# Last layer's first MLP product by pairs of tiles, seven block products each (Strassen's scheme), in a two-layer fp32 transformer step

## The chip, the core and the metric

The kernel runs on one core of a Trainium2 chip. The metric is the device time of one execution in microseconds (us): three executions of the kernel before gave 1744.67, 1745.09 and 1748.14, a median of 1745.09. Engines are named as in the profile: PE (matmul), PEld (its weight loads), DVE (VectorE), ACT (ScalarE), POOL (GpSimd) and SP (which issues the weight loads from HBM).

## The reference, cut to what matters

Two layers of a hybrid attention and gated-linear-attention block act on 640 columns of activations: 512 latent columns and 128 prompt columns, model width 1024. All is fp32. The end of each layer is an MLP of width 4096; the change is in its first product, in the last layer:

```
h = rmsnorm(x, g_mlp[l]) * (1 + sc2) + sh2
x = x + ga2 * mlp(h, w_up[l], w_down[l])

def mlp(h, w_up, w_down):
    return jnp.square(jax.nn.relu(h @ w_up)) @ w_down
```

## The kernel before, in words

**Tiles.** Activations lie transposed: eight row chunks of 128 partitions, each 640 columns wide (T, line 19). A weight unit is one load of 128x1024 fp32 (512 KB). An "up" unit is w_up for 128 of the 4096 hidden rows, all eight chunks of the contraction. A "dn" unit is w_down for 512 hidden rows (four up tiles) and 256 output rows. The last layer has 32 units of each kind.

**Three products for one.** To keep fp32 accuracy every operand is split into a rounded part and a remainder, and `mm3` (line 547) issues three matmuls for each product: rounded weight by rounded activation, rounded weight by remainder, remainder weight by rounded activation. The 640 columns (642 in an up product, whose last two carry the shift sh2 through the product) are done in two parts, 256 and 384 (or 386), so an up unit is 8 x 3 x 2 = 48 matmuls (`proj`, line 596), and a dn unit twice 24 (`proj4`, line 693), once for each of its 128 output rows.

**Preparing a unit.** `prefetch` (line 421) runs each time a unit has been used (`used`, line 490). It issues the next load on SP while fewer than NRAW = 3 raw tiles (wr) are held, and prepares the next raw tile while fewer than NHL = 3 prepared tiles (wh, wl) are held: ACT copies it to the rounded wh, POOL subtracts to make the remainder wl.

**Around the MLP of the last layer.** `layer` (line 867) ends with the output projection ("o" units). As each row chunk of x gets its last contribution (`resid`, DVE), `late_chunk` (line 836) scales it by G into the rounded row (ACT) and the remainder row (DVE), and adds its square to sqa (ACT, then DVE). PE sums sqa over partitions (ps_ss, in `late_stat`, line 853) and ACT makes rstd2 of it, the factor that is multiplied in when an up product leaves PSUM. The first two up tiles are run side by side (`proj_two`, line 577), the others one by one. An up tile leaves PSUM by `up_evac` (line 1569): DVE multiplies by rstd2 into r, ACT applies the shift and the relu and squares to uh, DVE makes the remainder ul. Buffers r have four turns. PSUM holds two tiles "mm" of two banks and four tiles "sm" of one; accumulators take them in turn.

**Order.** `unit_order` (line 377) sets it: in the MLP four up units, then the four dn units that use the four up tiles before them, and so on. PE's order is the order of the code; on the other engines a scheduler places the instructions by priority, and each engine runs its own in that order.

Of the kernel before, what the change touches and what calls it, by code (L numbers as in the profile page):

```python
# [20 lines left out]
TX = T + 2  # L21
NS = 512
L = 2
# [188 lines left out]
class Kern:  # L212
# [4 lines left out]
    EVP = 600  # L217
    HALF = ((0, 256), (256, T))
# [7 lines left out]
    def run(self):  # L226
        nc, a, ctx = self.nc, self.a, self.ctx
        self.cp = cp = ctx.enter_context(self.pool("const"))
        self.rp = ctx.enter_context(self.pool("rows"))
# [24 lines left out]
        self.cos = cp.tile([128, NS], F32, name="cos")  # L254
        self.sin = cp.tile([128, NS], F32, name="sin")
# [3 lines left out]
        self.cbc = cp.tile([128, 2, D], F32, name="cbc")  # L259
        self.ones = cp.tile([128, 128], F32, name="ones")  # L260
        self.blk_r = cp.tile([128, 128], F32R, name="blk_r")
        self.wg = cp.tile([128, L, 2, 256], F32, name="wg")
        self.xs = self.dp.tile([KC, 128, T], F32, name="xs")
        self.mod = {l: cp.tile([128, 6, KC, 2], F32, name=f"mod{l}") for l in range(L)}
        self.lateh = False
# [7 lines left out]
        self.raw, self.hl, self.over = {}, {}, set()  # L273
        self.rot, self.nacc = False, 0
# [102 lines left out]
    def unit_order(self):  # L377
# [8 lines left out]
        for l in range(L):  # L386
# [34 lines left out]
    def prefetch(self, ahead=650):  # L421
        nc = self.nc
        with self.tc.high_priority(offset=ahead):
            go = True
            while go:
# [35 lines left out]
                if self.raw and self.wprep - self.wused < (self.NHL if self.wx is None else self.NHL + 1):  # L461
                    j = min(self.raw)
                    wx = self.wx is not None and self.wprep == self.NHL
                    t = self.raw.pop(j)
                    if wx:
                        h, lo = (self.wx.tile([128, 1024], F32R, name=n) for n in ("wxh", "wxl"))
                    else:
                        h = self.wp.tile([128, 1024], F32R, name="wh", tag="wh", bufs=self.NHL)
                        lo = self.wp.tile([128, 1024], F32R, name="wl", tag="wl", bufs=self.NHL)
                    self.est.ready[t.name] = max(self.est.ready[t.name], self.dv.t)  # L470
                    nc.scalar.activation(out=h, in_=t, func=AF.Copy)
                    if self.wx is not None:
                        nc.vector.tensor_tensor(out=lo, in0=t, in1=h.bitcast(F32), op=ALU.subtract)
                    elif self.units[j] in self.units[max(0, j - 4):j] + self.units[j + 1:j + 5]:

                        nc.vector.tensor_tensor(out=lo[:, :448], in0=t[:, :448], in1=h[:, :448].bitcast(F32), op=ALU.subtract)
                        nc.gpsimd.tensor_tensor(out=lo[:, 448:], in0=t[:, 448:], in1=h[:, 448:].bitcast(F32), op=ALU.subtract)
                    else:
                        nc.gpsimd.tensor_tensor(out=lo, in0=t, in1=h.bitcast(F32), op=ALU.subtract)
                    self.hl[j] = (h, lo)  # L480
                    self.wprep += 1
                    go = True
# [7 lines left out]
    def used(self, i):  # L490
        self.over.add(i)
        if self.units[i][0] == "ada":
            self.nada -= 1
        elif self.units[i][0] != "z":
# [28 lines left out]
    def acc(self, n=T):  # L523
        t = self.mmp.tile([128, 1024], F32, name="ps_mm", tag="mm")
        return (t[:, 256:512], t[:, 512:256 + n]), [(t[:, 256:256 + n], 0, n)]

    def acc_sm(self, n=T):
        self.dv.take("sm", 2)
        a, b = (self.smp.tile([128, 512], F32, name="ps_sm", tag="sm") for _ in range(2))
        return (a[:, 0:256], b[:, 0:n - 256]), [(a[:, 0:256], 0, 256), (b[:, 0:n - 256], 256, n)]  # L530
# [16 lines left out]
    def mm3(self, ps, wh, wl, hh, hl, first, last, halves=(0, 1), shared=None):  # L547

        nc = self.nc
        for i, (w, h) in enumerate(((wh, hh), (wh, hl), (wl, hh))):  # L550
            for hf in halves:
                lo = self.HALF[hf][0]
# [43 lines left out]
    def proj(self, key, evac):  # L596

        n = TX if self.lateh else T
# [85 lines left out]

    def whole(self, t, segs, np_=128):

        nc = self.nc
        for ap_, lo, hi in segs:
            nc.vector.tensor_tensor(out=t[:, lo:hi], in0=ap_, in1=self.lrstd[0:np_, lo:hi], op=ALU.mult)
# [1044 lines left out]
```

## Time and profile before

| | before |
|---|---|
| three executions, median | 1745.09 us |
| the profiled execution, its own time | 1745.39 us |
| span of the profiled execution | 1743.6 us |
| mean granted clock of PE | 0.979 |
| PE busy, of the span | 95% |
| DVE busy, of the span | 62% |
| ACT busy, of the span | 40% |
| POOL busy, of the span | 36% |

A line of the profile names the tile written, the tiles read, the size and the engine. Nearly all instructions carry one line number, that of a helper, so groups are told apart by tiles. Ends of matmuls are modelled; the time that a matmul takes from the stream is the distance between starts.

### The profile page before, as it was taken

Reading aid. Unit: us, or ns where it says so; the run is one execution under the profiler, and the core shown is the slowest. Engines: PE = TensorE matmul, PEld = TensorE weight load, DVE = VectorE, ACT = ScalarE, POOL = GpSimd, SP = SyncE. Lnnn points to the kernel's source line nnn. Section 1 sums busy time; section 2 is a strip of 40 time slices with the busy share of each in tenths; the row PEclk is TensorE's granted clock in tenths of the full one; section 3 lists DMA queues with packets and bytes.
Section 4 is the critical chain, followed back from the end, with each engine's and each line's share of the span. In section 5 each row is a group of like instructions: output and inputs, shape, how many; then the busy total and the mean of one; then the engine's idle time right before and its main releaser. Section 6 shows DMA issues by size and latency. Waiting matters only on the chain. (4 is left out here: it accounts for less than half of the span.)

```text
span 1743.6 us, 32610 instructions
## 1 busy us (share of the span) xinstructions
PE 1653.4 (95%) x13712; PEld 1575.1 (90%) x13712; DVE 1076.4 (62%) x1971; ACT 703.3 (40%) x1142; POOL 626.7 (36%) x266
## 2 busy tenths in 40 slices
PE   7988788989999999999989899999999999999999
PEld 6977677779999999999988788888999999999998
DVE  5686767788797788777677737586662222222322
ACT  3535335543543233322344445466454223332330
POOL 1234432113334444444345536313233333333331
PEclk9998899999999999999999989999999999999999
DMA  9121233233354454445241111323222222222221
GB/s 369 45 65 64 92 105 119 77 110 121 121 181 139 157 166 134 144 147 169 76 168 51 51 43 57 91 69 94 70 65 84 73 73 73 74 83 74 73 73 73
DMA packets 61345, 179.28 MB, mean 103 GB/s; under 512 B 6928, under 2 KB 17808, under 8 KB 61200
## 3 DMA queue, kind: packets, MB, share of 16 engines
q1 hardware_dynamic: 45360, 159.76, 27.4%
q10 hardware_dynamic: 15840, 17.45, 3.2%
q8 instruction: 108, 1.77, 0.4%
q14 instruction: 37, 0.30, 0.1%
HBM read 170.36 MB, written 6.82 MB: 102 GB/s over the span
## 5 line engine op out<-in xcount | busy, mean ns | idle before, releaser
L197 POOL TENSOR_TENSOR wl<-wr,wh 128x1024 fp32r<-128x1024 f32 (+1 forms) x188 | 490.1, 2608 | 906.0 <-ACT wh L197 856.5
L197 PE MATMUL ps_mm<-row,wh 128*128 128x256 f32 (+1 forms) x2416 | 485.8, 322 | 7.9 <-DVE row L197 3.7
L197 ACT ACTIVATE wh<-wr 128x1024 fp32r<-128x1024 f32 x195 | 206.3, 1058 | 627.7 <-PE ps_sm L197 400.7
L197 PEld LDWEIGHTS ps_mm<-row,wh 128*128 128x128 f32 x2416 | 399.7, 193 | 30.3 <-issue 18.7
L197 PE MATMUL ps_mm<-row,wl 128*128 128x256 f32 (+2 forms) x1208 | 282.7, 313 | 0.5 <-DVE wl L197 0.5
L197 PEld LDWEIGHTS ps_mm<-row,wl 128*128 128x128 f32 x1208 | 224.8, 192 | 0.9 <-DVE wl L197 0.7
L197 DVE SCALAR_TENSOR_TENSOR row<-ps_sm,mod,row 128x256 f32<-128x256 f32 (+1 forms) x216 | 81.8, 432 | 97.0 <-PE ps_sm L197 97.0
L197 DVE SCALAR_TENSOR_TENSOR row<-ps_mm,mod,row 128x128 f32<-128x128 f32 (+2 forms) x180 | 89.4, 536 | 79.2 <-PE ps_mm L197 79.0
L197 DVE SCALAR_TENSOR_TENSOR ar<-ar,cbc 128x1024 f32<-128x1024 f32 x56 | 122.7, 2199 | 0.8
L197 ACT ACTIVATE r<-r 128x640 f32<-128x640 f32 (+2 forms) x192 | 112.3, 617 | 18.6 <-DVE r L197 15.1
L197 PE MATMUL ps_sm<-uh,wh 128*128 128x256 f32 (+1 forms) x512 | 119.2, 309 | 0.0
L197 PE MATMUL ps_mm<-uh,wh 128*128 128x256 f32 (+1 forms) x512 | 119.2, 309 | 0.0
L197 PE MATMUL ps_mm<-ul,wh 128*128 128x256 f32 (+1 forms) x512 | 119.0, 309 | 0.0
L197 PE MATMUL ps_sm<-uh,wl 128*128 128x256 f32 (+1 forms) x512 | 118.9, 309 | 0.0
L197 PE MATMUL ps_sm<-ul,wh 128*128 128x256 f32 (+1 forms) x512 | 118.9, 309 | 0.0
L197 PE MATMUL ps_mm<-uh,wl 128*128 128x256 f32 (+1 forms) x512 | 118.9, 309 | 0.0
L197 PE MATMUL ps_sm<-row,wh 128*128 128x256 f32 (+1 forms) x624 | 118.6, 309 | 0.0
L197 DVE TENSOR_TENSOR ul<-r,uh 128x640 fp32r<-128x640 f32 x64 | 55.2, 862 | 84.5 <-ACT r L197 84.4
L197 DVE TENSOR_TENSOR r<-ps_mm,rstd 128x642 f32<-128x642 f32 x34 | 28.1, 827 | 123.7 <-PE ps_mm L197 123.7
L197 PEld LDWEIGHTS ps_sm<-row,wh 128*128 128x128 f32 x624 | 103.0, 189 | 0.0
L197 PE MATMUL ps_mm<-m,wh 128*128 128x256 f32 (+1 forms) x544 | 102.3, 310 | 0.0
L197 DVE SCALAR_TENSOR_TENSOR r<-ar,cbc 128x1024 bf16<-128x1024 f32 x56 | 93.6, 1689 | 0.0
(203 smaller groups left out, 2947.1 us busy)
## 6 DMA issues: line engine op xcount, KB each, us to landing
wr<-w_dn SPq DMA_DIRECT2D x68, 512.0 KB, 3.5
wr<-w_up SPq DMA_DIRECT2D x64, 512.0 KB, 3.5
ar<-w_ada SPq DMA_DIRECT2D x56, 512.0 KB, 3.7
wr<-w_in SPq DMA_DIRECT2D x48, 512.0 KB, 3.5
wr<-w_ada SPq DMA_DIRECT2D x24, 512.0 KB, 3.5
wa<-w_ada SPq DMA_DIRECT2D x16, 512.0 KB, 10.2
wr<-w_o SPq DMA_DIRECT2D x16, 512.0 KB, 3.5
tab<-bias ACTq DMA_DIRECT2D x32, 96.0 KB, 2.2
```

The costliest lines, as they stand in the source:

```text
L197: r = f(*args, **kw)
```

## The change

Of the 32 up tiles of the last layer the first four stay as they are. The other 28 are taken in 14 pairs. For a pair the two weight units are seen as a 2 x 2 block matrix (two tiles of 128 hidden rows by two halves of the contraction), the activations as 2 x 2 blocks (two halves of the contraction by two halves of the columns, 322 each, for which TX becomes 644), and the product of the two is made with seven block products in place of eight, in Winograd's form of Strassen's scheme.

- `proj_pair` issues the seven products, 12 matmuls of 322 columns each, and combines them on DVE as they leave PSUM (p1, q, r and so on).
- `prepare_part` makes the weights of a pair as four prepared tiles in place of two: the first unit as it lies, two sums S1 and S2 in one tile, the first unit changed in place, and half a tile. Three are 1024 columns wide, the last 512; remainders go to POOL and DVE by turns. Sums are made on DVE.
- `blocks_begin` makes the four combined activation blocks T1 to T4, for four chunk pairs, once, at the start of the last layer's MLP: ACT scales x again into r, DVE subtracts, ACT rounds, DVE makes the remainder.
- In the last layer pairs and dn units alternate (two up units, two dn units); r there has three turns (RBUF).
- In both layers an up product's shift columns move to the two ends of the row, two each, and its two parts are 322 and 322. Constants of the attention move to a pool that is closed before the last MLP. Code of the case `lateh` in the projections, which was never taken there, goes.

```diff
-TX = T + 2
+TX = T + 4
+TH = TX // 2
...
+    PAIRED = (1,)
+    RBUF = (4, 3)
...
+                if l in self.PAIRED and 0 < b < 8:
+                    for i in (0, 2):
+                        for kind, j in (("up", 4 * b), ("dn", 4 * b - 4)):
+                            put(kind, l, j + i)
+                            put(kind, l, j + i + 1)
+                    continue
...
+    def prepare_part(self, j):
...
+            nc.vector.tensor_tensor(out=s1, in0=a21, in1=a22, op=ALU.add)
+            nc.vector.tensor_tensor(out=s2, in0=s1, in1=a11, op=ALU.add)
+
+            self.part = [j, 0, (ta, sums, ta, a22), ((a11, a21), (a12, s2))]
+        j, q, parts, late = self.part
+        if q == 2:
+            for t, u in late:
+                nc.vector.tensor_tensor(out=t, in0=t, in1=u, op=ALU.add)
+        t = parts[q]
+        n = t.free_size()
...
+        nc.scalar.activation(out=h[:, :n], in_=t, func=AF.Copy)
+        eng = nc.vector if q % 2 else nc.gpsimd
+        eng.tensor_tensor(out=lo[:, :n], in0=t, in1=h[:, :n].bitcast(F32), op=ALU.subtract)
...
+    def blocks_begin(self, l, x, mp, rc, rows):
...
+        for k in range(4):
+            b = []
+            for kc in (k, k + 4):
+                t = mp.tile([128, TX], F32, name="r", bufs=self.RBUF[l])
+                for c, e in ((1, 0), (0, T + 2)):
+                    nc.vector.tensor_copy(t[:, e:e + 2], m[:, 3, kc, c:c + 1].to_broadcast([128, 2]))
+                for c, lo, hi in ((1, 0, NS), (0, NS, T)):
+                    nc.scalar.activation(out=t[:, 2 + lo:2 + hi], in_=x[kc][:, lo:hi], func=AF.Copy, scale=self.G[:, kc, c:c + 1])
+                b.append(t)
+            (b11, b12), (b21, b22) = ((hv(t, 0), hv(t, 1)) for t in b)
+
+            for out, y, z in ((b11, b12, b11), (b12, b12, b22), (b22, b22, b11), (b21, b21, b22)):
+                nc.vector.tensor_tensor(out=out, in0=y, in1=z, op=ALU.subtract)
+            for i, t in enumerate((b11, b22, b12, b21)):
+                hh, hl = next(room), next(room)
+                nc.scalar.activation(out=hh, in_=t, func=AF.Copy)
+                nc.vector.tensor_tensor(out=hl, in0=t, in1=hh.bitcast(F32), op=ALU.subtract)
+                self.T[i].append((hh, hl))
+
+    def proj_pair(self, l, i, mp):
...
+        def mul(ps, w, n, rhs):
+            for kc in range(4):
+                ws = slice(512 * n + 128 * kc, 512 * n + 128 * kc + 128)
+                for k, (wv, hv) in enumerate(((w[0], rhs[kc][0]), (w[0], rhs[kc][1]), (w[1], rhs[kc][0]))):
+                    nc.tensor.matmul(ps, lhsT=wv[:, ws], rhs=hv, start=kc == k == 0, stop=kc == 3 and k == 2)
...
+        yield from mul(X, w, 0, B11)
+        with self.tc.high_priority(offset=self.EVP):
+            nc.scalar.activation(out=p1, in_=X, func=AF.Copy)
+        yield from mul(Y, w, 1, B21)
+        tt(ha[0], Y, p1, ALU.add)
...
+        yield from mul(X, w, 0, T2)
+        tt(q, X, p1, ALU.subtract)
+        yield from mul(Y, w, 1, T1)
+        tt(r, Y, q, ALU.add)
...
+        yield from mul(V, w, 0, T3)
+        tt(hb[1], V, r, ALU.add)
+        tt(q, V, q, ALU.add)
...
+        yield from mul(W, w, 1, B22)
+        tt(ha[1], W, r, ALU.subtract)
...
+        yield from mul(V, w, 0, T4)
+        tt(hb[0], V, q, ALU.add)
```

How the order moves, at the three places of which the prediction speaks.

PE, one chunk of one of the last up tiles, before: each product in two parts, rows as they are named in the text above (row_0 is the rounded part of the first chunk, row_1 its remainder).

```order
L197 MATMUL ps_mm<-row_0_13329,wh 128x256
L197 MATMUL ps_mm<-row_0_13329,wh 128x386
L197 MATMUL ps_mm<-row_1_13330,wh 128x256
L197 MATMUL ps_mm<-row_1_13330,wh 128x386
L197 MATMUL ps_mm<-row_0_13329,wl 128x256
L197 MATMUL ps_mm<-row_0_13329,wl 128x386
```

PE, the last pair with the change, from the end of its second block product to the begin of its third.

```order
L198 MATMUL ps_mm<-m_13364,wh 128x322
L198 MATMUL ps_mm<-m_13365,wh 128x322
L198 MATMUL ps_mm<-m_13364,wl 128x322
L198 MATMUL ps_mm<-T_13719,wh 128x322
L198 MATMUL ps_mm<-T_13720,wh 128x322
L198 MATMUL ps_mm<-T_13719,wl 128x322
```

What moved: a chunk's three products of one part stand alone, for one block; a pair has 84 matmuls where two up tiles had 96, and the whole program has 11558 where it had 11726.

DVE, start of the last layer's MLP, before: the last chunk (row_7) gets its contribution, its remainder m, the square sum, and then the first two up tiles leave PSUM (r<-ps_mm).

```order
L197 SCALAR_TENSOR_TENSOR row_7_12735<-ps_sm,mod_108,row_7_12735 128x256 x2
L197 SCALAR_TENSOR_TENSOR row_7_12735<-ps_sm,mod_108,row_7_12735 128x128
L197 SCALAR_TENSOR_TENSOR m_13344<-row_7_12735,G,m_13343 128x512
L197 SCALAR_TENSOR_TENSOR m_13344<-row_7_12735,G,m_13343 128x128
L197 TENSOR_TENSOR sqa<-sqa,sq 128x640
L197 TENSOR_TENSOR r<-ps_mm,rstd_4521 128x642 x2
```

DVE, the same place, with the change: T is a combined block, r<-r a subtraction between scaled chunks, COPY r<-mod the shift columns. The square sum is the row sqa; after the last row shown 17 more rows of these kinds stand before r<-ps_mm of the first up tile.

```order
L198 SCALAR_TENSOR_TENSOR row_7_12755<-ps_sm,mod_111,row_7_12755 128x256 x2
L198 SCALAR_TENSOR_TENSOR row_7_12755<-ps_sm,mod_111,row_7_12755 128x128
L198 TENSOR_TENSOR T_13722<-r,T_13721 128x322
L198 TENSOR_TENSOR T_13724<-r,T_13723 128x322
L198 SCALAR_TENSOR_TENSOR m_13365<-row_7_12755,G,m_13364 128x512
L198 SCALAR_TENSOR_TENSOR m_13365<-row_7_12755,G,m_13364 128x128
L198 TENSOR_TENSOR sqa<-sqa,sq 128x640
L198 COPY r<-mod_111 128x2 x4
L198 TENSOR_TENSOR r<-r 128x322 x3
L198 TENSOR_TENSOR S_13941<-wr 128x512
L198 TENSOR_TENSOR r<-r 128x322
L198 TENSOR_TENSOR S_13941<-S_13941,wr 128x512
```

What moved: two remainders T stand ahead of the last chunk's remainder m, and work on the blocks fills the place between the square sum and the first up tile's way out of PSUM.

ACT, a pair in the steady part of the last MLP, before (one up unit, whose weight copy is wh<-wr, then r and uh of an up tile):

```order
L197 ACTIVATE wh<-wr 128x1024
L197 ACTIVATE r<-r 128x512
L197 ACTIVATE r<-r 128x128
L197 ACTIVATE uh_14121<-r 128x640
L197 ACTIVATE r<-r 128x640
L197 ACTIVATE wh<-wr 128x1024
```

ACT, the same part with the change, one pair; wh<-S is the sums' tile, wh<-wr of 512 columns the last half tile, r<-ps_mm the copy of the first block product out of PSUM. The two wh<-wr of 1024 columns right behind the half tile are the two dn units that follow the pair.

```order
L198 ACTIVATE wh<-wr 128x1024
L198 ACTIVATE r<-ps_mm 128x322
L198 ACTIVATE wh<-wr 128x512
L198 ACTIVATE wh<-wr 128x1024 x2
L198 ACTIVATE r<-r 128x512
L198 ACTIVATE wh<-wr 128x1024
L198 ACTIVATE r<-r 128x128
L198 ACTIVATE uh_14454<-r 128x640
L198 ACTIVATE r<-r 128x640
L198 ACTIVATE r<-r 128x512
L198 ACTIVATE r<-r 128x128
L198 ACTIVATE uh_14485<-r 128x640
```

What moved: the copies for weights stand closer together, and those for the dn units wait for PE inside the pair.

## Rows read from the trace of the kernel before

**Rows 1.** The page's busy time of PE (share of the span, instructions).

```profile
PE 1653.4 (95%) x13712; PEld 1575.1 (90%) x13712; DVE 1076.4 (62%) x1971; ACT 703.3 (40%) x1142; POOL 626.7 (36%) x266
```

**Rows 2.** Busy time by stretch: length, PE, PEld, DVE, ACT, POOL, PEclk, DMA share, GB/s.

```profile
1262.00:1293.00 31.00, 30.52 (x207) 30.07 (x205) 24.97 (x43) 17.18 (x29) 9.62 (x4) 1.00 0.25 81
1429.00:1485.00 56.00, 56.00 (x384) 56.00 (x383) 15.22 (x30) 18.33 (x24) 19.21 (x8) 1.00 0.23 76
```

**Rows 3.** Chain of waits, last MLP: start, length, what ran, matmuls.

```profile
1436.28 7.06 PE ps_sm L197 x48
...
1457.46 3.51 PE ps_mm L197 x24
1460.97 3.52 PE ps_sm L197 x24
```

**Rows 4.** Timeline of PE, first layer's last dn units: start, length, operation.

```profile
884.73 0.28 PE L197 MATMUL ps_sm<-ul,wh 128*128 128x256 f32 x1
...
888.72 0.28 PE L197 MATMUL ps_sm<-uh,wl 128*128 128x256 f32 x1
...
897.06 0.34 PE L197 MATMUL ps_mm<-ul,wh 128*128 128x384 f32 x1
...
905.21 0.34 PE L197 MATMUL ps_mm<-uh,wh 128*128 128x384 f32 x1
```

**Rows 5.** Groups by form from 1293 us on: busy, mean ns, idle before.

```profile
L197 POOL TENSOR_TENSOR wl<-wr,wh 128x1024 fp32r<-128x1024 f32 x61 | 146.5, 2402 | 284.7 <-ACT wh L197 284.7
L197 ACT ACTIVATE wh<-wr 128x1024 fp32r<-128x1024 f32 x61 | 64.7, 1061 | 278.5 <-PE ps_sm L197 206.8 <-PE ps_mm L197 71.7
...
L197 DVE TENSOR_TENSOR r<-ps_sm,rstd 128x386 f32<-128x386 f32 x15 | 8.3, 551 | 0.0
L197 DVE TENSOR_TENSOR r<-ps_sm,rstd 128x256 f32<-128x256 f32 x15 | 6.4, 425 | 39.1 <-PE ps_sm L197 39.1
```

**Rows 6.** DMA issues: operation, count, KB each, median us to landing.

```profile
wr<-w_up SPq DMA_DIRECT2D x64, 512.0 KB, 3.5
```

**Rows 7.** Timeline of DVE around the square sum and the first up tiles.

```profile
1287.82 1.13 DVE L197 SCALAR_TENSOR_TENSOR row<-ps_sm,mod,row 128x256 f32<-128x256 f32 x3
1289.48 1.81 DVE L197 SCALAR_TENSOR_TENSOR m<-row,G,m 128x512 fp32r<-128x512 f32 x2 [0.54 <-ACT m L197]
1291.21 0.81 DVE L197 TENSOR_TENSOR sqa<-sqa,sq 128x640 f32<-128x640 f32 x1
1300.59 0.83 DVE L197 TENSOR_TENSOR r<-ps_mm,rstd 128x642 f32<-128x642 f32 x1 [8.56 <-PE ps_mm L197]
```

**Rows 8.** Timeline of PE there: first up tile, square sum, third up tile.

```profile
1286.13 0.75 PE L197 MATMUL ps_mm<-row,wh 128*128 128x256 f32 x4
...
1292.08 1.34 PE L197 MATMUL ps_ss<-sqa,ones 128*128 128x256 f32 x4 [0.48 <-DVE sqa L197]
...
1302.09 0.75 PE L197 MATMUL ps_mm<-row,wh 128*128 128x256 f32 x4
```

**Rows 9.** Timeline of DVE in the output projection.

```profile
1266.71 2.61 DVE L197 SCALAR_TENSOR_TENSOR row<-row,G,row 128x512 fp32r<-128x512 f32 x2 [0.53 <-ACT row L197]
1269.24 0.81 DVE L197 TENSOR_TENSOR sqa<-sqa,sq 128x640 f32<-128x640 f32 x1
```

**Rows 10.** Timeline of POOL in the output projection, and its slowest remainder in the first layer.

```profile
422.06 3.33 POOL L197 TENSOR_TENSOR wl<-wr,wh 128x1024 fp32r<-128x1024 f32 x1 [0.84 <-ACT wh L197]
...
1266.11 2.40 POOL L197 TENSOR_TENSOR wl<-wr,wh 128x1024 fp32r<-128x1024 f32 x1 [4.65 <-ACT wh L197]
...
1288.07 2.41 POOL L197 TENSOR_TENSOR wl<-wr,wh 128x1024 fp32r<-128x1024 f32 x1 [4.92 <-ACT wh L197]
```

**Rows 11.** Timeline of PE, first layer: waits at the same place, and one of 2.75 us.

```profile
452.23 0.83 PE L197 MATMUL ps_mm<-row,wh 128*128 128x256 f32 x4 [1.48 <-DVE row L197]
458.53 1.34 PE L197 MATMUL ps_ss<-sqa,ones 128*128 128x256 f32 x4 [1.63 <-DVE sqa L197]
...
893.31 0.70 PE L197 MATMUL ps_ss<-sqa,ones 128*128 128x256 f32 x2 [2.75 <-DVE sqa L197]
...
894.02 0.34 PE L197 MATMUL ps_mm<-ul,wh 128*128 128x384 f32 x1
```

**Rows 12.** Timeline of DVE, first layer: two of the shift columns' small operations.

```profile
421.28 0.16 DVE L197 TENSOR_TENSOR row<-mod,row 128x2 fp32r<-128x2 f32 x1
421.36 0.16 DVE L197 CAST row<-mod 128x2 fp32r<-128x2 f32 x1
```

More of the change, by code (lines that the diff above doesn't have):

```diff
@@ L462, in prefetch @@
                     j = min(self.raw)
[L463 to L479, printed above, removed]
@@ L480, in prefetch, with prepare @@
-                    self.hl[j] = (h, lo)
-                    self.wprep += 1
-                    go = True
+                    if self.part is None and not self.paired(self.units[j]):
+                        self.prepare(j)
+                        go = True
+                    elif self.part is not None or j + 1 in self.raw:
+                        self.prepare_part(j)
+                        go = True
+    def prepare(self, j):
+        nc = self.nc
+        wx = self.wx is not None and self.wprep == self.NHL
+        t = self.raw.pop(j)
+        if wx:
+            h, lo = (self.wx.tile([128, 1024], F32R, name=n) for n in ("wxh", "wxl"))
+        else:
+            h = self.wp.tile([128, 1024], F32R, name="wh", tag="wh", bufs=self.NHL)
+            lo = self.wp.tile([128, 1024], F32R, name="wl", tag="wl", bufs=self.NHL)
+        self.est.ready[t.name] = max(self.est.ready[t.name], self.dv.t)
+        nc.scalar.activation(out=h, in_=t, func=AF.Copy)
+        if self.wx is not None:
+            nc.vector.tensor_tensor(out=lo, in0=t, in1=h.bitcast(F32), op=ALU.subtract)
+        elif self.units[j] in self.units[max(0, j - 4):j] + self.units[j + 1:j + 5]:
+            nc.vector.tensor_tensor(out=lo[:, :448], in0=t[:, :448], in1=h[:, :448].bitcast(F32), op=ALU.subtract)
+            nc.gpsimd.tensor_tensor(out=lo[:, 448:], in0=t[:, 448:], in1=h[:, 448:].bitcast(F32), op=ALU.subtract)
+        else:
+            nc.gpsimd.tensor_tensor(out=lo, in0=t, in1=h.bitcast(F32), op=ALU.subtract)
+        self.hl[j] = (h, lo)
+        self.wprep += 1
@@ new lines, in prepare_part @@
+    def prepare_part(self, j):
+        nc = self.nc
+        if self.part is None:
+            ta, tb = self.raw[j], self.raw[j + 1]
+            for t in (ta, tb):
+                self.est.ready[t.name] = max(self.est.ready[t.name], self.dv.t)
+            sums = self.sw.tile([128, 1024], F32, name="S12")
+            a11, a12, a21, a22 = ta[:, 0:512], ta[:, 512:1024], tb[:, 0:512], tb[:, 512:1024]
+            s2, s1 = sums[:, 0:512], sums[:, 512:1024]
+            nc.vector.tensor_tensor(out=s1, in0=a21, in1=a22, op=ALU.add)
[7 more added lines that the diff above has]
+        n = t.free_size()
+        h = self.wp.tile([128, 1024], F32R, name="wh", tag="wh", bufs=self.NHL)
+        lo = self.wp.tile([128, 1024], F32R, name="wl", tag="wl", bufs=self.NHL)
+        nc.scalar.activation(out=h[:, :n], in_=t, func=AF.Copy)
+        eng = nc.vector if q % 2 else nc.gpsimd
+        eng.tensor_tensor(out=lo[:, :n], in0=t, in1=h[:, :n].bitcast(F32), op=ALU.subtract)
+        self.hl[j, q] = (h, lo)
+        self.wprep += 1
+        self.part[1] += 1
+        if q == 2:
+            self.raw.pop(j)
+        elif q == 3:
+            self.raw.pop(j + 1)
+            self.part = None
@@ L488, in unit, with used_part, used @@
         return i, self.hl.pop(i)
-    def used(self, i):
-        self.over.add(i)
-        if self.units[i][0] == "ada":
+    def used_part(self):
+        self.wused += 1
+        self.prefetch()
+    def used(self, *i):
+        self.over.update(i)
+        if self.units[i[0]][0] == "ada":
             self.nada -= 1
-        elif self.units[i][0] != "z":
+        elif self.units[i[0]][0] != "z" and len(i) == 1:
             self.wused += 1
@@ L967, in layer @@
         rows += [tuple(mp.tile([128, TX], F32R, name=f"m{i}{j}", bufs=1) for j in range(2)) for i in range(4)]
-        self.h, self.lateh = rows, True
+        self.h = rows
+        if l in self.PAIRED:
+            self.sw = self.mlp_ctx.enter_context(self.pool(f"blocks{l}", reuse_waits="tile"))
         with self.pool(f"norm2_{l}", 2, reuse_waits="tile") as npl:
@@ L1608, in mlp @@
                 self.ups = []
-            if b < 8:
+            if b < 8 and not self.paired(("up", l, 4 * b)):
                 for i in range(len(self.ups), 4):
```

206 lines of the change are left out of this document (119 added, 87 removed).

## The prediction

> **What bounds the kernel now.** I read the page first: PE is busy 95% of the span [rows 1]. Whether it bounds the stage that is changed is read from the busy times by stretch: between 1429 and 1485 us, four up and eight dn units deep in the last MLP, PE is busy 56.00 of 56.00 us at a granted clock of 1.00, while DVE has 15, ACT 18 and POOL 19 us of work [rows 2]. The chain of waits says the same: from 1293 us to the end it is PE alone, 7.06 us for each up unit (48 matmuls) and 3.51 or 3.52 us for each half of a dn unit (24) [rows 3]. So a matmul taken out of this stage is worth its full time, as long as nothing new makes PE wait. The stage before it is another matter. In the output projection (1262 to 1293 us) DVE is busy 24.97 of 31 us [rows 2], and it is late: the last chunk's contribution starts on DVE at 1287.82 us [rows 7], though PE left the output projection for the first up tile at 1286.13 [rows 8]. PE waits for DVE's square sum at 1292.08 already, for 0.48 us [rows 8]. The change puts new DVE work just there.
>
> **The matmuls.** Matmuls of 256 columns alone start 117.4 ns apart (34 steps from 884.73 to 888.72 us), those of 384 columns 173.4 ns (47 steps from 897.06 to 905.21) [rows 4]. On the line between them 322 columns take 117.4 + 66 x 56.0/128 = 146.3 ns. A pair of up tiles takes 2 x 7.06 = 14.12 us before [rows 3], and 84 x 146.3 ns = 12.29 us after: 1.83 us less, **25.6 us for 14 pairs**. The other bound: today's mixed stream has 7.06 us / 48 = 147.1 ns for a mean of 321 columns; with 147.5 ns for 322, a pair saves 1.73 us, 24.2 in all. I take the line, since the new stream is of one size, as the streams it comes from are. The Trainium skill (TensorE: Matmul & The Clock Gate, section Back-to-back issue gap) gives N/2.4 + 2.5 ns for an isolated gap; by it the pairs would save only 22.4 us, an estimate from that page, and the trace disagrees with it already at 256 columns (109.2 ns against the measured 117.4).
>
> The other 36 up tiles (32 in the first layer, 4 in the last) go from parts of 256 and 386 columns to 322 and 322. By the same line each matmul falls from 147.1 to 146.3 ns: 36 x 48 x 0.8 ns = **1.4 us less**; by the other bound 0.7 us more. The dn units keep their matmuls; that they alternate with pairs moves no work off or onto PE.
>
> **The weights of a pair.** Four prepared tiles in place of two: ACT copies 3.5 tile widths where it copied 2, POOL keeps two remainders of 2.40 us per pair [rows 5], DVE gets the other two, four sums of 512 columns, seven combinations of 322 and two full-width products by rstd2. All lie beside PE if each tile is ready in time. With three prepared tiles, the copy for a tile starts when the tile three places earlier has been used. The shortest lead is that of the first dn unit: its copy waits for the pair's second part, and PE comes to it after the third and fourth, 36 matmuls or 5.27 us later. Copy and remainder take 1.06 + 2.40 = 3.46 us [rows 5], so 1.8 us are left; POOL's slowest remainder in the rows here, 3.33 us [rows 10], would still leave 0.9. A half tile's lead is 7.0 us, the third part's too, the others' are longer. Loads: a pair holds two of the three raw tiles until its third and fourth part are prepared, and the copy of the second dn unit stands 7.1 us behind the end of the third part's preparation (72 matmuls or 10.5 us into the pair, against 3.46), against 3.5 us to landing [rows 6]. DVE's row of work waits in front of the next pair's first sum until its second raw tile lands (some 2 us into the first dn unit), and the last block product's combination stands behind it; nobody needs that result for over 20 us. I take **0**, with an upper bound of 0.5 us per pair, 7 in all: one two-input DVE operation of 0.81 us [rows 7] ahead of POOL's 3.33. Below nothing is excluded, since PE does not wait there now.
>
> **The blocks T.** This is the cost that I do not take for hidden. An operation of 322 columns is not in the trace; DVE's of 256 and 386 take 425 and 551 ns [rows 5], so about 0.49 us alone, and 0.41 in a row, as the square sum of 640 columns takes 0.81 but the next starts 0.73 after it. Two steps follow.
>
> Ahead of the square sum DVE gets ten such operations, 4.1 us. It waits about 0.53 us before each chunk's remainder for ACT's rounded copy [rows 7, 9]; by the order four of the ten fall into such a gap, so 2.5 us stay. Then POOL: while it runs, a DVE operation with two inputs in SBUF stands still. At 1266.71 us a remainder that takes about 1.0 us took 2.61, starting 0.60 us into POOL's 2.40 and ending 0.8 behind it [rows 9, 10]. The Trainium skill (SBUF — State Buffer, section Who interferes with whom) states this as an exclusive lock; by that rule, the trace agrees. Before, POOL's last remainder in this stage ran from 1288.07 to 1290.48 [rows 10]. Its copy on ACT now stands behind six more operations; placing the chunks one after the other with these durations I get it from 1291.7 to 1294.1, and the last chunk's T remainders and its own remainder wait for its end: 2.1 us more. The square sum's matmul comes at 1296.7 in place of 1292.1: **4.6 us**. (Part of it PE spends earlier, since the second up tile's PSUM is freed by the seventh chunk's contribution, late by 3 us; it is the same wait.)
>
> Behind the square sum 19 operations of 0.41, two sums of 512 columns at 0.6 and ten small copies at 0.08 (small operations start 0.08 apart [rows 12]) stand before the first up tile's way out of PSUM: 7.8 + 1.2 + 0.8 = 9.8 us, and the 0.8 of that step itself [rows 7]; with about 1 us of waiting for ACT in between, 11.6 us from 1296.7, thus 1308.3. The third up tile takes over that PSUM tile. PE, with the same work as before, reaches it 4.6 us later than the 1302.1 us of rows 8, at 1306.7, and waits 1.6. Together **6.2 us**, where DVE had 8.56 us of idle time to give before [rows 7].
>
> Bounds: with every gap filled (eight, 0.41 each) and no wait at POOL the first step costs 0.8 and the second 0.4, 1.2 us in all; with no gap filled, two POOL operations in the way (4.1 + 4.8) and half a microsecond lost at each of a dozen hand-overs to ACT, about 15. A drop of the clock I leave out: after PE's wait of 2.75 us at 893.31, longer than either wait here is expected to be in one piece, its next matmuls run at full pace [rows 11].
>
> **Shift columns.** 16 casts and 16 remainders of two columns more in each layer, 0.08 us apart: 2.6 us of DVE work in each. The first layer has the same two waits for DVE as the last, 1.48 and 1.63 us [rows 11], so some could show; most stand between operations that wait for POOL anyway. I take **0.3 us**, bounds 0 and 5.
>
> **Sum.** -25.6 - 1.4 + 6.2 + 0.3 = -20.5 against the profiled execution's own 1745.39 us: 1724.9. That execution is 0.3 us above the median, so about **1724.6, say 1725 us**, 1.2% less. A measurement of this kernel can tell about 0.2% (3.5 us) from no change.
>
> **The rivals.**
> *The blocks are hidden.* If the new operations fall into DVE's gaps, the lower bound of 1.2 us holds: 1745.1 - 27.0 + 1.2 + 0.3 = 1719.6 us. For it: DVE's 8.56 us idle. Against it: DVE is late already in the projection. 0.13.
> *The blocks cost their upper bound, or some weights come late.* 15 us in place of 6.2, or up to 0.5 us per pair: 1732 to 1741 us. For it: buffers r have three turns now, and eight scaled chunks pass through them, each waiting for DVE and ACT in turn. 0.17.
> *The weights become the bound: slower.* The same lock has another side: a DVE operation that starts first keeps POOL waiting. The order lets only PSUM-reading operations come near the first dn unit's remainder, which do not collide; but if the products by rstd2 and the sums slid there, four of 0.81 ahead of a 3.33 us remainder and the copy make 7.6 us against the 5.27 at hand: 2.3 us per pair, 33 us in all, 1758 us. From 1.46 us per pair on (20.5/14) the gain is gone. Against it: 0.9 us of slack with the slowest remainder, and POOL has one third of the stretch. 0.04.
> *The pairs do not shorten PE*, because 322 columns from an offset of half a row cost more than the line says. At 84 against 96 matmuls the gain is gone when one takes 146.3 + 20500/1176 = 164 ns, nearer to what 384 columns take than the line puts it [rows 4]. 0.02.
> The forecast itself, with the blocks between 3 and 11 us: 0.64.
>
> **How the numbers follow.** Faster by over 0.2% is below 1741.6: the forecast, the hidden blocks and nearly all of the costly ones, 0.93. Slower by over 0.2%: 0.04. The rest, 0.03. The range takes in the hidden blocks (1719.6, less a microsecond for the line) and the costly ones up to 15 us with the dearer matmul in the pairs, 1725 + 8.8 + 1.4, rounded up: **1718.5 to 1736 us**.
>
> **What would show it.** Right: in the chain of waits a pair shows 84 matmuls in about 12.3 us and an up tile 7.02; PE busy without a gap from the first pair on; a wait of PE for sqa, or for the seventh chunk, of 4 to 5 us together, and one of about 2 us before the third up tile; POOL's slowed DVE rows around 1292 us. Wrong: waits of PE for wl or wr in every period, a matmul spacing above 148 ns in pairs, or the square sum on time.

## The result, and the profile after

Eight executions of the changed kernel took 1750.31 to 1758.30 us, with a median of 1755.82; eight of the kernel before had a median of 1745.29. The ratio is 1.0057, with a 95% interval of 1.0040 to 1.0073: **slower by about 10 us, where 20 us less were forecast**, and outside the range. The profiled execution took 1757.89 us (span 1756.0, mean granted clock 0.973).

Busy time by stretch, changed kernel (the columns of [rows 2]). In the first line DVE is busy 26.54 of 27 us and PE is not; in the second, deep in the pairs, PE no longer fills the stretch, where before it was busy 56.00 of 56 [rows 2].

```profile
1293.00:1320.00 27.00, 22.75 (x138) 21.69 (x137) 26.54 (x58) 20.81 (x42) 6.43 (x3) 0.94 0.11 40
1429.00:1485.00 56.00, 53.77 (x363) 52.70 (x363) 33.38 (x55) 22.31 (x30) 20.59 (x9) 1.00 0.24 76
```

The chain of waits over one period (a pair, then two dn units), changed kernel; it answers to [rows 3].

```profile
1389.63 1.80 PE ps_mm L198 x12
...
1391.46 0.45 ACT r L198
...
1391.95 3.84 PE ps_mm L198 x24
...
1395.82 0.50 DVE r L198
...
1396.36 2.06 PE ps_mm L198 x12
1398.42 5.34 PE ps_sm L198 x36
1403.76 3.46 PE ps_mm L198 x24
1407.21 3.44 PE ps_sm L198 x24
...
1417.53 1.80 PE ps_mm L198 x12
```

A pair takes 1403.76 - 1389.63 = 14.13 us, as much as two up tiles did (14.12). PE stops twice in it: behind the first product until ACT has copied it out of PSUM (0.45 us), and behind the third until DVE has combined it (0.50 us). The last three products, in tiles of their own, follow each other without a gap. A second thing in these rows: a dn half takes 3.44 us, where it took 3.51 or 3.52 [rows 3]. The waits of PE from the first pair to the end say the same twice over all 14 pairs (engine, tile, what was waited for: us in total, times, longest):

```profile
PE ps_mm L198 <- DVE r L198: 8.2, 14, 0.6
PE ps_mm L198 <- ACT r L198: 7.4, 14, 0.5
```

These 15.6 us go by the modelled ends of PE's matmuls. Its weight loads (PEld) wait 11.9 and 11.1 us at the same places, 23.0 together.

Where the waits are is in PE's order of the changed kernel too. These are the first matmuls of the first four products of a pair, with the semaphores that each waits for:

```
L198 MATMUL ps_mm<-row_0_13350,wh 128x322 [waits DVE_49,PE_49,Activation_49]
L198 MATMUL ps_mm<-m_13358,wh 128x322 [waits Activation_49]
L198 MATMUL ps_mm<-T_13719,wh 128x322 [waits DVE_49,PE_49]
L198 MATMUL ps_mm<-T_13717,wh 128x322 [waits DVE_49]
```

The second and the fourth have nothing new to read from ACT or DVE; they wait because X and Y are halves of one PSUM tile, and the program guards a tile as a whole. X and Y lie in different banks. The Trainium skill (PSUM — Partial Sum Buffer, section Summary: rules for kernel authors) asks for a semaphore by bank, and for matmuls to go to another bank than the one being read. By that rule these two waits need not be there. No run here has two products in one tile without the wait; the experiment below takes another tile.

PE's timeline of the changed kernel on the way into the last MLP answers to [rows 8], where the same events start at 1286.13, 1292.08 and 1302.09:

```profile
1297.64 0.75 PE L198 MATMUL ps_mm<-row,wh 128*128 128x322 f32 x4
...
1300.09 0.83 PE L198 MATMUL ps_mm<-row,wh 128*128 128x322 f32 x4 [1.41 <-DVE row L198]
...
1307.62 1.78 PE L198 MATMUL ps_ss<-sqa,ones 128*128 128x256 f32 x4 [2.84 <-DVE sqa L198]
1308.63 1.85 PE L198 MATMUL ps_mm<-row,wh 128*128 128x322 f32 x4
...
1319.31 0.76 PE L198 MATMUL ps_mm<-row,wh 128*128 128x322 f32 x4
```

From the first up tile to the third 21.67 us pass, where 15.96 passed before. The waits, 1.41 and 2.84 us, are those that the prediction named; the third tile itself waits for nothing. But the four matmuls behind the square sum take 1.85 us, as many elsewhere 0.75. The granted clock (third from the right, as in [rows 2]) says why; in the kernel before it was 1.00 from 1286 to 1302 us.

```profile
1308.00:1312.00 4.00, 4.00 (x16) 3.46 (x14) 3.97 (x10) 3.23 (x8) 0.00 (x0) 0.57 0.03 10
```

By stages, from starts of matmuls in PE's timelines of the profiled executions (us):

| stage | before | after | own_tiles | straight | best_safe |
|---|---|---|---|---|---|
| to the first layer's first up tile | 449.7 | 449.8 | 449.0 | 447.8 | 449.2 |
| from there to the square sum behind a long wait (2.75 us in [rows 11], 3.04 in best_safe) | 443.6 | 448.0 | 448.2 | 448.1 | 438.9 |
| on to the last layer's first up tile | 392.8 | 399.8 | 397.0 | 395.8 | 398.5 |
| its first four up tiles | 30.1 | 36.0 | 36.1 | 30.4 | 35.7 |
| from the fifth up tile or first pair to the end | 427.4 | 422.4 | 399.7 | 425.8 | 399.7 |
| span | 1743.6 | 1756.0 | 1729.9 | 1747.9 | 1722.0 |

(The last three columns are experiments.) The pairs and all behind them gave 5.0 us in place of 25.6, as much as the faster dn halves alone (64 x 0.08). The third line holds attention and gated attention, which the change hardly touches; it takes 392.2 to 399.8 us in the profiles shown here and in the other experiments (392.8 to 396.9 in the kernel before and its variants), and is no measure of anything below 7 us.

### The profile page after: what moved, and what is told of

The parts are those of the page before. It is cut to its first block, busy times and chain, and to the rows that moved or that the text cites. A ratio compares the mean times of both kernels' runs of the same rounds, so it can differ in the third digit from the quotient of the medians.

```text
span 1756.0 us, 32676 instructions
## 1 busy us (share of the span) xinstructions
PE 1645.5 (94%) x13544; PEld 1556.9 (89%) x13544; DVE 1226.2 (70%) x2220; ACT 744.6 (42%) x1216; POOL 635.4 (36%) x266
## 5 line engine op out<-in xcount | busy, mean ns | idle before, releaser
L198 POOL TENSOR_TENSOR wl<-wr,wh 128x1024 fp32r<-128x1024 f32 (+1 forms) x188 | 499.5, 2661 | 909.2 <-ACT wh L198 869.3
L198 PE MATMUL ps_mm<-row,wh 128*128 128x256 f32 (+2 forms) x2416 | 496.8, 323 | 10.3 <-DVE row L198 5.9
L198 ACT ACTIVATE wh<-wr 128x1024 fp32r<-128x1024 f32 (+1 forms) x209 | 214.9, 1028 | 539.6 <-PE ps_sm L198 212.2
L198 PE MATMUL ps_mm<-row,wl 128*128 128x384 f32 (+2 forms) x1208 | 292.0, 313 | 0.5 <-DVE wl L198 0.5
L198 ACT ACTIVATE r<-r 128x512 f32<-128x512 f32 (+2 forms) x192 | 113.8, 618 | 61.6 <-DVE r L198 58.9
L198 PE MATMUL ps_sm<-row,wh 128*128 128x322 f32 (+2 forms) x512 | 102.9, 312 | 0.0
L198 PE MATMUL ps_mm<-m,wh 128*128 128x322 f32 x432 | 87.3, 315 | 7.4 <-ACT r L198 7.4
L198 PEld LDWEIGHTS ps_sm<-ul,wh 128*128 128x128 f32 x512 | 92.9, 189 | 0.1
L198 PEld LDWEIGHTS ps_sm<-uh,wh 128*128 128x128 f32 x512 | 92.8, 189 | 0.1
L198 PEld LDWEIGHTS ps_sm<-uh,wl 128*128 128x128 f32 x512 | 92.8, 189 | 0.0
```

The lines of the kernel that those rows point to most:

```text
L198: r = f(*args, **kw)
```

## Experiments

Ratios are to the kernel before, run on the same chip; the changed kernel has 1.0057. A difference of 0.01 in them is 17.5 us.

**own_tiles: a PSUM tile for each product.**

```diff
-        X, Y = a[:, 0:TH], a[:, 512:512 + TH]
+        X = a[:, 0:TH]
...
+        Y = small()
         yield from mul(Y, w, 1, B21)
         tt(ha[0], Y, p1, ALU.add)
+        dv.rel("sm", 1, self.est.free(Y))
```

(and the same for b.)

> Edit: in a pair, the second and the fourth product (Y of both PSUM tiles) go to a one-bank tile of their own, as the last three do. Theory A (a product waits until the one before it, in the same PSUM tile, has been read out): in the profile after, a pair takes 14.13 us, of which 84 matmuls at the 148.3 ns of the last 36 make 12.46; the other 1.67 us go. The period of a pair and two dn units falls from 27.90 to 26.2 us, the run by 14 x 1.67 = 23 us to 1732 us, faster than before. Rival B (prepared weights come late, or DVE's row of work): the waits move to wh, wl or r, the period stays above 27.5 and the run near 1755 us.

Measured: 1730.13 us, ratio 0.9918 (0.9901 to 0.9936), 24 us below the changed kernel. The chain of waits of own_tiles, one pair and the first half of the dn unit behind it:

```profile
1409.20 1.79 PE ps_mm L198 x12
1410.99 1.80 PE ps_sm L198 x12
1412.79 1.77 PE ps_mm L198 x12
1414.57 7.13 PE ps_sm L198 x48
1421.70 3.46 PE ps_mm L198 x24
```

A pair takes 12.50 us, and neither PE nor its weight loads wait for anything from the first pair to the end. Theory A holds; the prepared weights are in time, so rival B falls, and with it the forecast's rival in which weights become the bound.

**third_wait: one shared tile more.** The fifth and sixth product share a two-bank tile (c) as X and Y do.

```diff
-        V = small()
+        c = self.mmp.tile([128, 1024], F32, name="ps_mm", tag="mm")
+        V, W = c[:, 0:TH], c[:, 512:512 + TH]
         yield from mul(V, w, 0, T3)
```

> Edit: the fifth and sixth product share one two-bank PSUM tile too, so that a third product of a pair stands behind a read-out. Theory A: the read-out here is two DVE operations in a row, about 1.0 us with the hand-over, and 0.3 us of slow restart as at the other two waits: 1.3 us per pair, 18 us in all, 1774 us. Rival B (weights or DVE late): the new wait is covered by the old ones, 1756 us.

Measured: 1767.70 us, ratio 1.0140 (1.0117 to 1.0163), 14 us above the changed kernel. The chain of waits of third_wait, from one pair's third stop to the next pair's, which stands behind two DVE operations:

```profile
1395.92 2.04 PE ps_mm L198 x12
...
1413.54 1.80 PE ps_mm L198 x12
...
1415.86 3.84 PE ps_mm L198 x24
...
1420.27 3.84 PE ps_mm L198 x24
...
1424.13 0.90 DVE r L198 x2
...
1425.08 2.05 PE ps_mm L198 x12
```

The period from one such stop to the next is 1425.08 - 1395.92 = 29.16 us against 27.90, 1.26 more, 17.6 in 14 pairs. One stop costs its read-out and 0.3 to 0.4 us more (1.26 - 0.90 here, 0.82 - 0.45 and 0.82 - 0.50 for the two in the changed kernel): the added wait shows in full, it is not covered.

**straight: the layout alone.** No pairs, no blocks.

```diff
-    PAIRED = (1,)
+    PAIRED = ()
```

> Edit: no pairs and no blocks (all 32 up tiles of the last layer one by one, four up and four dn units in turn as before); the layout of 644 columns, the parts of 322 and 322 and r's three turns stay. In the profile after, an up tile of the first layer takes 7.18 us against 7.06 before, a dn half of the last layer 3.44 against 3.52, and the last layer's fifth o unit starts 11.7 us later than before. Theory C (the layout costs what that profile shows ahead of the pairs): 64 x 0.12 - 64 x 0.08 + 11.7 - 32 x 0.12 = +10.4, about 1756 us. Theory D (the part of the 11.7 us that the up tiles do not explain is spread from run to run): +2.6, about 1748 us.

Measured: 1753.17 us, ratio 1.0054 (1.0033 to 1.0075). The layout alone makes the kernel about as slow as the change does. An up tile takes 7.18 us, as expected, in both layers. From the chain of waits of straight, last layer:

```profile
1441.87 7.18 PE ps_sm L198 x48
...
1463.41 3.45 PE ps_mm L198 x24
1466.86 3.44 PE ps_sm L198 x24
```

Which of C and D holds stays open: the run's median speaks for C, but in its profile (second column from the right in the table) 3.0 of the 4.3 us against before lie in the stretch that moves by itself.

**own_388 and straight_388: parts of 256 and 388.**

```diff
-        m = TH if n == TX else 256
+        m = 256
```

> Edit to own_tiles: up tiles that are not in pairs (32 in the first layer, 4 in the last) go in parts of 256 and 388 columns in place of 322 and 322. Theory I (two equal parts are slower on PE here: 7.18 us for an up tile in the profile after against 7.06 before, where the prediction's line gave 7.02): 36 x 0.12 = 4.3 us less, 1726 us. Theory J (the 7.18 come from something else that the layout brought): no change, 1730 us.

Measured: 1724.12 us, ratio 0.9877 (0.9858 to 0.9895); 7 us less than own_tiles, give or take 4.5 (both intervals reach 0.0018 to either side). The first layer's up tiles fall to 7.05 us. Theory I holds: it is the two equal parts.

> Edit to straight: parts of 256 and 388 columns in place of 322 and 322 in all 64 up tiles. Theory I (the equal parts are slower by 0.12 us a tile, as the profile after shows): 7.7 us less than straight, 1745.5 us; 0.17 us a tile, as own_388 gained on its 36, would make it 1742.5. What then stays against the kernel before is the price of the doubled shift columns and the rest of the layout, less 5 us for the last layer's faster dn halves. Theory J (the equal parts are not it): 1753 us.

Measured: 1750.04 us, ratio 1.0035 (1.0020 to 1.0051). The up tiles do fall, to 7.05 us, 64 x 0.13 = 8 us less, but this kernel's last layer has dn halves of 3.60 us, 64 x 0.16 = 10 us more than in straight. By these rows it should be no faster than straight; the runs have it 3 us faster, give or take 4.5. From its chain of waits:

```profile
1436.27 7.05 PE ps_sm L198 x48
...
1461.00 3.60 PE ps_sm L198 x24
```

**straight_320: where the second part starts.** Parts of 320 and 324 (m = TH - 2).

> Edit to straight: parts of 320 and 324 columns, so that the second part starts at a multiple of 64 bytes from the first. Theory O (the start of the second part, 1288 bytes behind the first, makes the up tiles slow): an up tile falls from 7.18 to 7.05 us. Theory P (two parts of nearly equal size are slower, wherever they start): it stays at 7.18 us, run about 1753 us.

Measured: an up tile takes 7.07 us, the number of theory O. But the edit changes the sizes together with the start, and the pairs speak against the start alone. In own_tiles the second product of a pair reads only parts that begin where their row begins (B21), the sixth only parts that begin 1288 bytes behind (B22): 12 matmuls of 322 columns each, on the rows m. PE's timeline of own_tiles, the first matmuls of the second, third, sixth and seventh product:

```profile
1410.83 0.46 PE L198 MATMUL ps_sm<-m,wh 128*128 128x322 f32 x2
...
1412.63 0.46 PE L198 MATMUL ps_mm<-T,wh 128*128 128x322 f32 x2
...
1417.97 0.46 PE L198 MATMUL ps_sm<-m,wh 128*128 128x322 f32 x2
...
1419.76 0.46 PE L198 MATMUL ps_sm<-T,wh 128*128 128x322 f32 x2
```

The second takes 1.80 us, the sixth 1.79. So whether the size of 322 or the start makes the equal parts slow stays open. The run took 1757.51 us (two executions, ratio 1.0078), as this kernel too has dn halves of 3.60 us.

**before_pad, before_pad64, before_rows, after_pad: where the moving operand starts.** In the built programs uh and ul start at 0, modulo 64 bytes, in both layers of the kernel before; in the last layer of the changed kernel at 32, as three buffers r of 2592 bytes stand before them in place of four.

```diff
         self.ups = []
+        mp.tile([128, 8], F32, name="pad", bufs=1)
```

(before_pad64: 16 columns; after_pad: in the last layer of the changed kernel alone.)

> Edit, in the kernel before: an unused tile of 32 bytes per partition ahead of r, so that every uh and ul of both layers starts 32 bytes further on (at 32 in place of 0, counted modulo 64); nothing else moves. Theory E (the address at which the moving operand starts sets the pace of dn products): a dn half falls from 3.52 to 3.44 us in both layers, 128 x 0.08 = 10 us, 1735 us. Rival F (the faster dn halves come from the alternation with pairs, or from r's three turns): no change, 1745 us.

Measured: 1732.93 us, ratio 0.9940 (0.9922 to 0.9958), 10.5 us less, by 32 unused bytes. From the chain of waits of before_pad, last layer:

```profile
1403.06 3.44 PE ps_mm L197 x24
1406.51 3.44 PE ps_sm L197 x24
...
1423.70 7.09 PE ps_mm L197 x48
```

> Edit, in the kernel before: the unused tile is 64 bytes, so uh and ul move by 64 and start at 0 again, counted modulo 64. Theory E as refined (the start modulo 64 bytes counts): dn halves stay at 3.52 us, run 1743.5 us. Rival H (any shift against the neighbours helps): as with 32 bytes, 3.44 us and 1733 us.

Measured: 1746.34 us, ratio 1.0006 (0.9994 to 1.0018), dn halves 3.52 us. Not the shift but the start modulo 64 counts.

```diff
-        rows = [self.pair_rows(ra, i, TX) for i in range(4)]
+        mp.tile([128, 8], F32, name="pad", bufs=1)
+        rows = [self.pair_rows(ra, i, T + 16) for i in range(4)]
```

> Edit, in the kernel before: rows and m get 656 columns (a pitch of a multiple of 64 bytes) and 32 bytes stand ahead of m, so that the operands of up, o and dn products all start at 32, counted modulo 64, where the rows took turns between 0 and 32 and uh, ul stood at 0. Theory E for every product: dn halves at 3.44 us (10 us less), and up tiles at dn's pace, 143.9 in place of 147.1 ns a matmul, 64 x 0.15 = 10 us less again: 1724 us. Rival N (it is dn's 256 and 384 alone, the up tiles' 386 do not follow): 1734 us.

Measured: 1740.68 us, ratio 0.9968 (0.9952 to 0.9984). The dn halves take 3.44 us, the up tiles 7.08: rival N for the pace, and a run some 6 us above its number. Of these, 1 us is the first layer's way to its third up tile (19.8 us against 18.8); where the rest lies stays open.

> Edit, in the changed kernel: an unused tile of 32 bytes in the last layer, so that its uh and ul start at 0 modulo 64 bytes, as they did before the change. Theory E (r's three turns moved them to 32, which made the dn halves faster by 0.08 us): the last layer's dn halves return to 3.52 us, 64 x 0.08 = 5 us more, 1761 us. Rival F (the faster dn halves come from the alternation with pairs): no change, 1756 us.

Measured: 1755.11 us, ratio 1.0061 (1.0044 to 1.0078). The chain of waits of after_pad has the old pace back:

```profile
1429.61 3.52 PE ps_sm L198 x24
```

From the first pair to the end its profile needs 427.7 us against 422.4, the 5 us of theory E. The run does not show them; its stretch ahead of the last MLP was 7.6 us shorter in this profile (392.2 us), the one that moves by itself.

**straight_388_b and straight_b: the same programs again.**

> No edit: straight_388 once more, for the pace of the last layer's dn halves in its profile, 3.60 us there against 3.44 in straight, though every operand stands at the same address. If the kernel sets it: 3.60 us again. If it differs from execution to execution: another of the values seen (3.44 or 3.52).

> No edit: straight once more, for the pace of the last layer's dn halves in its profile, 3.44 us at first. If the kernel sets it: 3.44 us again. If it differs from execution to execution: another of the values seen (3.52 or 3.60).

Measured: 3.60 us again, and 3.44 again (1748.85 and 1754.13 us, one execution each). The kernel sets the pace, not the execution. But the dn matmuls of these two kernels stand at the same addresses, operand by operand; they differ in the up tiles' parts alone. So the start modulo 64 is one condition and not the only one. What else decides between 3.44 and 3.60 stays open.

**own_noblocks and own_late: the price and the place of the blocks.**

```diff
+        self.T = [[self.B[i % 2][kc + i // 2 * 4] for kc in range(4)] for i in range(4)]
+        return
```

> Edit to own_tiles: the blocks T1 to T4 are not made; the products read the plain blocks of h in their place, so the up products of the pairs are left uncomputed as such. Theory K (the blocks cost what lies between the fifth o unit and the third up tile, 49.6 us in the profile after against 44.1 before, and 5.7 us more in own_tiles between the first and the third up tile): 5.6 us less, 1724.5 us. Theory L (DVE's other work would hold PE there anyway, since shift columns and an already late square sum remain): under 2 us less, 1729 us.

Measured: 1725.38 us, ratio 0.9888 (0.9872 to 0.9903), 5.2 us below own_tiles, give or take 4; in its profile the first four up tiles take 30.4 us again, 5.6 less than in own_tiles. Theory K holds: the blocks cost some 5.5 us.

own_late makes the blocks behind the fourth up tile and puts two dn units ahead of the first pair:

```diff
-                        for kind, j in (("up", 4 * b), ("dn", 4 * b - 4)):
+                        two = (("up", 4 * b), ("dn", 4 * b - 4))
+                        for kind, j in two[::-1] if b == 1 else two:
```

> Edit to own_tiles: the blocks are made behind the first four up tiles in the program's order, and the first pair comes after two dn units (up 0 to 3, two dn, pair, two dn, pair, pair, and so on as before), so that DVE has them behind the square sum. Theory K with their place as the cause: the wait for the square sum goes, 4 to 5.6 us less, 1725 us. Rival M (the blocks only move their wait: to the first pair's second product, which needs T2, or the two pairs in a row wait for weights): 1730 us or more.

Measured: 1738.63 us, ratio 0.9976 (0.9960 to 0.9992), 10 us above own_tiles: rival M. The waits of PE in own_late, from 1285 us on, in this form as above:

```profile
PE ps_mm L198 <- ACT row L198: 3.8, 2, 3.2
PE ps_mm L198 <- DVE row L198: 1.9, 2, 1.5
PE ps_mm L198 <- ACT uh L198: 1.8, 1, 1.8
PE ps_mm L198 <- DVE ul L198: 1.8, 1, 1.8
```

The square sum is nearly on time, and PE waits for the blocks (in rows) and for the last up tiles instead. In its chain a sum S, on DVE, first waits for a raw tile's load (4.16 us from 1315.27), with the up tiles' remainders queued behind it.

**best_safe and best_late: the parts that helped, together.** best_safe is own_388 with 32 bytes in the first layer, and one operation for both ends of a row's shift columns.

```diff
-            for c, e in ((1, 0), (0, T + 2)):
-                s = sh[:, c:c + 1].to_broadcast([128, 2])
-                nc.vector.tensor_copy(hh[:, e:e + 2], s)
...
+            s = sh[:, :, None].to_broadcast([128, 2, 2])
+            nc.vector.tensor_copy(eh, s)
```

> Edit to own_388: an unused tile of 32 bytes in the first layer, so that its uh and ul start at 32 too, modulo 64; and one DVE operation for both shift columns of a row in place of two (32 fewer small operations in each layer). By theory E 64 x 0.08 = 5 us less; by the first layer's third up tile, which starts 19.9 us behind the first in the profile after against 18.9 before, another 1 us: 1718 us. Rival (the shift columns cost nothing that shows): 1719 us.

Measured: **1721.89 us, ratio 0.9854 (0.9838 to 0.9870)**, the fastest, 1.5% less than before. Of the 5 to 6 us expected 4 came, give or take 4. Some of its gain is not the scheme's: before_pad, whose dn halves have the same pace, stands at 0.9940, so the pairs, with their blocks and their layout, are worth 0.0086, 15 us, beside it.

```diff
+            self.filler(self.proj_two([("up", l, i) for i in range(2)], up_ev))
             if l in self.PAIRED:
                 self.blocks_begin(l, x, mp, rc, rows)
-            self.filler(self.proj_two([("up", l, i) for i in range(2)], up_ev))
```

> Edit to best_safe: the blocks stand behind the first two up tiles in the program's order (the order of units stays), so that DVE makes them behind the square sum, while PE does the third and fourth up tile. Theory K with their place as the cause: own_noblocks gained 4.7 us, of which 4 should show here: 1714 us. Rival M (as in own_late: they hold up the way out of the third up tile and T2, and PE waits in front of the first pair): 1718 us or more.

Measured: 1726.49 us, ratio 0.9888 (0.9875 to 0.9901), 6 us above best_safe. The first four up tiles take 30.3 us again, and the wait moves to the first pair, as the waits of PE in best_late from 1284 us on show:

```profile
PE ps_mm L198 <- DVE r L198: 5.7, 1, 5.7
PE ps_mm L198 <- DVE row L198: 1.2, 1, 1.2
```

The blocks are DVE work that has to be done before the first pair. None of the three places tried hides it; that no other place would is not shown.

## Why the prediction was wrong, step by step

**The matmuls of the pairs: the step that failed.** The prediction said "PE busy without a gap from the first pair on", and took 25.6 us for 84 matmuls in a row. It went through weights, loads, POOL's lock and DVE's queue, and not through the PSUM tiles of the products themselves, though it lists the seven combinations and the order has the waits. Two stops of 0.82 us a pair, (14.13 - 12.50) / 2, are 23 us: own_tiles gets them back, third_wait adds one more. The price of a matmul was nearly right: without the stops a pair takes 12.50 us, where the line said 12.29 and the dearer bound 12.39. That is 148.8 ns a matmul, just over the 148 that the prediction named as a sign of being wrong, but it is 3 us in 14 pairs and not the step that failed.

**The other up tiles.** Forecast 1.4 us less, by the same line; in fact 7.18 against 7.06, 36 x 0.12 = 4.3 us more. The line through 256 and 384 columns gave 146.3 ns for 322, and the dearer bound 147.5; the runs have 148.8 in a pair (12.50 / 84) and 149.6 in an up tile (7.18 / 48), so the term and its bound of +0.7 were both too small. Parts of 320 and 324, or of 256 and 388, do not cost that; whether the size of 322 or the start of the second part does stays open. The isolated gap of the Trainium skill (TensorE: Matmul & The Clock Gate, section Back-to-back issue gap) would give 136.7 ns for 322 columns, an estimate from that section; the streams here, with a weight load for each matmul, are slower than that.

**The dn units** "keep their matmuls". They do, and became faster by 0.08 us a half: 64 x 0.08 = 5 us that nobody had put into the sum. They came with r's three turns in place of four, which moved uh and ul to 32 modulo 64 (after_pad, before_pad).

**The weights of a pair**: right at 0. The waits from the first pair on name neither wl nor wr, and in own_tiles, without the two stops, there are none at all.

**The blocks**: 6.2 us forecast, 5.2 (own_noblocks) to 5.7 (21.67 - 15.96) measured. Of the two steps the first is right: up to the square sum 9.98 us pass (1297.64 to 1307.62) where 5.95 did, 4.0 more, where 4.6 were forecast. The second is wrong: the third up tile does not wait. That its 1.6 us are nearly met is luck. From the square sum to the third up tile 11.69 us pass where 10.01 did, and these 1.7 us are in the main the clock's, which stood at 0.57 between 1308 and 1312 us.

**Shift columns**: 0.3 us forecast. From the first to the third up tile the first layer takes 19.9 us against 18.8, but before_rows, without the doubling, 19.8. Not resolved.

**The clock**, left out as PE ran at full pace after a wait of 2.75 us [rows 11] and no wait here was to be longer. One was, 2.84 us, and the clock fell behind it, as just said. It fell in the first layer too. Behind the same wait, as long (2.75 us, until 897.88), busy time by stretch of the changed kernel, in the columns of [rows 2]:

```profile
896.00:900.00 4.00, 2.12 (x8) 1.89 (x9) 3.00 (x7) 1.78 (x3) 1.79 (x2) 0.85 0.39 131
900.00:904.00 4.00, 4.00 (x19) 4.00 (x18) 0.79 (x4) 2.12 (x4) 0.23 (x1) 0.72 0.63 213
```

The granted clock is 0.85 and then 0.72 of full speed, so for part of the time 1.2 GHz and not 2.4, and 24.63 us pass to the next such sum (897.88 to 922.51) where 23.05 did (893.31 to 916.36). One row at full pace showed that the clock need not fall; the prediction read it as that it does not. This fall is not the change's own: before_pad and before_pad64, which have none of it, show it too (24.67 and 24.68 us to the next sum), and straight_388 does not (23.04).

**The sum**, with what was measured: 0 for the pairs, +4.3 - 5.1 + 5.6 = about +5 us. The runs say about 10, between 7 and 12.7. What is left, 2 to 8 us, has the 1.6 us of the first layer's clock in it. In the profiles, 7.0 of the 12.4 us between the two spans lie in the table's third line, which moves by as much from kernel to kernel; it is not settled.

**The rivals.** The slower one gave 1758 us, close to the result, but by late weights; own_tiles shows that none is late. A number that fits is no mechanism. No rival had a wait inside the pair.

## What to carry to other kernels

When a product's accumulators are cut out of one PSUM tile, ask at every product who reads the tile it writes, and look for that wait in the order before summing matmuls: here two read-outs of half a microsecond, 0.8 us each with stop and restart, ate the whole gain of one matmul in eight. Give each product a tile of its own. And when a layout changes, compare the pace of products that were not touched: a start address is part of the change.

## What the hardware showed that was not expected

A matmul's pace can depend on where its moving operand starts in SBUF. The dn halves (12 matmuls of 256 columns, 12 of 384) take 3.52 us in every layer of every kernel here whose uh and ul start at 0 modulo 64 bytes. At 32 they take 3.44 in all but the last layers of straight_388 and straight_320, where it is 3.60. The start is no general key, though: when before_rows moved the up tiles' rows to 32, they took 7.08 us, against 7.06. An up tile in parts of 322 and 322 takes 7.18 us, in parts of 320 and 324 it takes 7.07, in parts of 256 and 388 it takes 7.05; whether size or start does that is not settled. The two kernels that were run again showed the same values. Why the start counts, and what makes 3.60 of 3.44, no run here tells. 32 unused bytes were worth 10.5 us to the kernel before.
